# Dealing the mLSTM steps of a hybrid encoder block out at four places of a projection instead of one

## Chip, cores and metric

The kernel runs on one core of one Trainium2 chip. The time is the device time of one execution in microseconds, and 875.85 us is the median of three runs before the change (875.55 to 876.28).

## What is computed

One layer of a bidirectional encoder block on 512 tokens of width 1024, in fp32. From the normalised input come one combined projection, three token mixers (a chunkwise mLSTM in both directions, a 2-D neighbourhood attention, a cross-attention into 256 memory tokens), a gated merge, an output projection and a convolutional GLU feed-forward network. Cut to what the change touches:

```
h = rms_norm(x, mix_norm_g)
proj = h @ w_in      # mLSTM q,k,v,o,gates | attention q,k,v | memory q | merge gates
...
# mLSTM, one direction, per head and chunk: a = cumsum(log_f), D = a_j - a_s + log_i
m_j = max(a + m_prev, max_s D)
P = exp(D - m_j) * (q @ k.T)
num = P @ v + inter_w * (C_prev @ q)
den = sum(P) + inter_w * (n_prev @ q)
h = num / max(abs(den), exp(-m_j))
...
y_ml = sigmoid(o) * norm(h_fw + h_bw)
merged = g_ml * (y_ml @ w_br_ml) + g_na * (y_na @ w_br_na) + g_xa * (y_xa @ w_br_xa)
```

## The kernel before, in words

**Projections.** Every large matmul is done on a high and a low part of each operand: `mm3` (L212) issues three matmuls for each of the 8 tiles of 128 inputs, so a projection of 128 outputs for 512 tokens is 24 matmuls into one PSUM bank. `proj` (L395) does one such projection. Its weights come through `weights` (L201): SP loads blocks of 512 KB up to three ahead into three raw buffers, and one block ahead each block is split in two halves, the high part by ScalarE (L195, `wh`), the low part by VectorE (L196, `wl`). Four buffers of each kind hold two blocks, so a half can be split when its half of two blocks before is consumed. A raw buffer is free for SP's next load when its two L196 are done.

**Steps.** Between the projections the mLSTM is worked off in steps. `ml_all` (L652) is a generator whose `yield`s cut it in 27 pieces; `step(n)` (L1064) adds n to a quota and runs one piece for each whole number in it. Before the change a step call stands at the end of each projection, after its eviction from PSUM: `RB` = 1.25 for each of 16 projections in four groups of four (memory queries `xaq` L1080, output gates `o` L1086, neighbourhood queries and keys `naq`, `nak` L1119 and L1124), `RM` = 0.7 for eight shorter pieces of the memory keys and values between the second and third group. The gate projections that follow give half a step at their fourth tile and half at their end.

**What the pieces hold.** Piece 2: the transposes of the gate logarithms (L583) and the four scans over the tokens on VectorE (L589 to L601), two for the running maximum and two for the running sum. Piece 4: their difference `rr` (L607), written by POOL's queue to a buffer `rd` in DRAM (L609). Piece 5: transposes of the maxima (L614), the copy `lfc` (L618), the first loads of `R`, which is `rd` spread over all partitions (L660, on SP), and the transposes of the keys of head 0 (L681). Piece 6: `states` (L711) of head 0, the matmuls of keys with weighted values (L722 and `mm3` on the tile `u`). Then, for each head, `weights_J` (L742: key-query product L748, the exponential of `R` on ScalarE L752, their product `E` on VectorE L753) and, one piece later, `values_J` (L756: L761, L763 and a `mm3`); in the last piece of a head the keys of the next one; then the next states. `emit_y` (L802) transposes a finished head (L806).

**Deferred operations.** Pieces put work that may wait in the list `late`; `flush` (L390) emits it, and `proj` calls `flush` after its second tile. Among it are `spread` (L621: the maxima at chunk ends by L627, small sums, the exponentials L644 to L646), `weigh` (L697: the values times the state weights, L700, L703, L704), the masks added to `R` (`mask`, L664) and the products at the edges (`edges`, L668: L673 exponentiates `R`, L675 multiplies).

**Order.** Each engine works its own instructions in a fixed order. Within the order in which the program text emits them, the compiler's scheduler may move instructions of one engine past each other, so the order on an engine is not that of the text. `mem_part` (L484) loads a piece of the memory tokens (`memT`, SP), squares it (L489), splits it (L219, L220) and sums (L496); it stands at the end of each `xaq` projection, before its step.

Of the kernel before, what the change touches and what calls it, by code (L numbers as in the profile page):

```python
# [29 lines left out]
RM, RB = 0.7, 1.25  # L30
# [80 lines left out]
def hybrid_block(ctx, tc, xg, xT, memT, wflat, vecs, gbias, nabias, outa, outb, outc):  # L111
# [14 lines left out]
    def nm(s):  # L126
        uid[0] += 1
        return f"{s}_{uid[0]}"

    def unit(dt=F32):  # L130
        return up.tile([P, UNIT], dt, tag="unit", name=nm("u"))

    def scr(n=512):
        return sp.tile([P, S], F32, tag="scr", name=nm("s"))[:, :n]
# [4 lines left out]
    def mmps():  # L139
        return mmp.tile([P, 512], F32, tag="mm", name=nm("mm"))  # L140
# [60 lines left out]
    def weights(key):  # L201

        i, _, n = BINDEX[key]
        while st["raw"] <= min(i + RAW_AHEAD, len(BLOCKS) - 1):
            emit_raw(st["raw"])
            st["raw"] += 1
        while st["split"] <= min(i + SPLIT_AHEAD, len(BLOCKS) - 1):
            emit_split(st["split"])
            st["split"] += 1
        return split.pop(i)  # L210

    def mm3(ps, lh, ll, rh, rl, start, stop):  # L212
        PE.matmul(ps, lh, rh, start=start, stop=False)  # L213
        PE.matmul(ps, lh, rl, start=False, stop=False)  # L214
        st["mm"] = PE.matmul(ps, ll, rh, start=False, stop=stop).ins  # L215
# [89 lines left out]
    def folded(acc, ntok):  # L305

        lo, hi = slice(0, P // 2), slice(P // 2, P)
        t, parts = scr(ntok), sp.tile([P, S], F32R, tag="scr", name=nm("s"))[:, :ntok]
        A.activation(t[lo], acc[hi], AF.Copy)
        V.tensor_tensor(t[lo], acc[lo], t[lo], op=ALU.add)  # L310
        A.activation(parts[lo], t[lo], AF.Copy)
        V.tensor_tensor(parts[hi], t[lo], parts[lo].bitcast(F32), op=ALU.subtract)
        return (parts,)

    def square_sums(parts, ntok):

        ps = atps()
        for i, p in enumerate(parts):
            st["mm"] = PE.matmul(ps[:, :ntok], onesr, p, start=i == 0, stop=i == len(parts) - 1).ins
        return ps  # L320

    def rstd_cols(ps, ntok, tag, n=D):

        nt = ntok // P
        v, junk = tiny(nt), scr(P)
        for t in range(nt):
            V.tensor_tensor_reduce(junk, ps[:, t * P:(t + 1) * P], ident, 1.0 / n, 0.0, ALU.mult, ALU.add,
                                   accum_out=v[:, t:t + 1])
        col = cp.tile([P, nt], F32, name=f"rc_{tag}")
        st["pool"] = G.tensor_tensor(col, v, nhalf[:, :nt], op=ALU.pow).ins  # L330
        return col

    def rstd_wide(ps, ntok, tag, n=D):

        v, y = scr(ntok), scr(ntok)
        rb = cp.tile([P, ntok], F32, name=f"rb_{tag}", tag=f"rb{ntok}", bufs=1) if tag else scr(ntok)
        A.activation(v, ps[:, :ntok], AF.Ln, scale=1.0 / n)
        A.activation(y, v, AF.Exp, scale=-0.5)
        V.scalar_tensor_tensor(v, ps[:, :ntok], -0.5 / n, y, op0=ALU.mult, op1=ALU.mult)
        V.tensor_tensor(v, v, y, op=ALU.mult)  # L340
        V.scalar_tensor_tensor(rb, v, 1.5, y, op0=ALU.add, op1=ALU.mult)
        return rb
# [3 lines left out]
    XH = [hx[k // 4 * 2][:, (k % 4) * S:(k % 4 + 1) * S] for k in range(KT)]  # L346
    XL = [hx[k // 4 * 2 + 1][:, (k % 4) * S:(k % 4 + 1) * S] for k in range(KT)]
# [42 lines left out]
    def flush():  # L390

        while late:
            late.pop(0)()

    def proj(key, XHs, XLs, n=S, at={}, ps=None):  # L395

        ws = weights(key)
        k0 = 0 if ps is None else 1
        if ps is None:
            ps = mmps()  # L400
        for k in range(k0, KT):
            mm3(ps[:, :n], ws[k][0], ws[k][1], XHs[k], XLs[k], k == 0, k == KT - 1)
            if k == 1:
                flush()
            if k in at:
                at[k]()
        return ps
# [35 lines left out]
    def x_norm():  # L443
        ps = square_sums(xsum, S)
        norm.extend([rstd_wide(ps, S, "x"), rstd_cols(ps, S, "x")])

    proj(("mlk", 0), XH, XL, ps=ps_k[0], at={3: x_norm})
    proj(("mlk", 1), XH, XL, ps=ps_k[1])
    rb, rc = norm
    SY.dma_start(gbf, gbias.partition_broadcast(P))  # L450
# [24 lines left out]
    for f in range(4):  # L475
        ps = ps_k[f] if f < 2 else proj(("mlk", f), XH, XL)
        silu2(kT, slice(f * S, (f + 1) * S), conv(ps, rb, "mlw", "mlb", 4 + f, 8))
# [6 lines left out]
    def mem_part(kp):  # L484

        t = scr()
        SY.dma_start(t.rearrange("p (k m) -> p k m", k=2), memT[:, 2 * kp:2 * kp + 2, :])
        sq = scr()
        A.activation(sq, t, AF.Square)  # L489
        for i in range(2):  # L490
            k = 2 * kp + i
            split_act(MH[k], ML[k], t[:, i * M:(i + 1) * M], vcol("mem_g", k))
            if k == 0:
                V.scalar_tensor_tensor(macc, sq[:, :M], EPS * D / P, sq[:, M:2 * M], op0=ALU.add, op1=ALU.add)
            elif k > 1:
                V.tensor_tensor(macc, macc, sq[:, i * M:(i + 1) * M], op=ALU.add)  # L496
# [7 lines left out]
    for c in range(3):  # L504
        n, nk = TMC[c], TMK[c]
        pss = [(mmps if c % 2 else atps)() for _ in range(NT)]
        for h in range(KT // nk):
            ws = weights(("tm", c, h))
            for t in range(NT):
                tsl = slice(t * P, (t + 1) * P)  # L510
                for k in range(nk):
                    kk = nk * h + k
                    ps = pss[t][:, :n]
                    mm3(ps, XH[kk][:, tsl], XL[kk][:, tsl], ws[k][0], ws[k][1], kk == 0, kk == KT - 1)
        for t in range(NT):
            ps = pss[t]
            if c == 0:
                V.scalar_tensor_tensor(Gt[:, t, :], ps[:, :16], rc[:, t:t + 1], gb, op0=ALU.mult, op1=ALU.add)
            if c < 2:
                o = 16 if c == 0 else 0  # L520
# [543 lines left out]
    def step(n=1):  # L1064
        quota[0] += n
        while quota[0] >= 1 and gens:
            try:
                next(gens[0])
                quota[0] -= 1
            except StopIteration:  # L1070
                gens.pop(0)
        if not gens:
            quota[0] = 0.0
# [2 lines left out]
    so = []  # L1076
    gens.append(ml_all())

    xq = unit()
    for f in range(4):  # L1080
        ps = proj(("xaq", f), XH, XL)
        V.tensor_tensor(xq[:, f * S:(f + 1) * S], ps, rb, op=ALU.mult)
        mem_part(f)
        step(RB)
    for f in range(4):
        ps = proj(("o", f), XH, XL)  # L1086
        t = scr()
        V.tensor_tensor(t, ps, rb, op=ALU.mult)
        A.activation(t, t, AF.Tanh, scale=0.5)
        if f == 0:  # L1090
            so.append(unit())
            msum = folded(macc, M)
        if f == 1:

            with tc.issue_after(st["mm"]):
                mps = square_sums(msum, M)
            mrb, mrc = rstd_wide(mps, M, "m"), rstd_cols(mps, M, "m")
        V.tensor_scalar(so[0][:, f * S:(f + 1) * S], t, 1.0, None, op0=ALU.add)
        step(RB)
    mkv = unit()  # L1100
    mk, mv = mkv[:, 0:1024], mkv[:, 1024:2048]
    for f in range(4):
        ps = proj(("memk", f), MH, ML, M)
# [13 lines left out]
    nq, nk = unit(), unit()  # L1117
    rv = lambda a: a.rearrange("p (r b c) -> p b r c", r=ROWS, b=4)
    for f in range(4):  # L1119
        ps = proj(("naq", f), XH, XL)  # L1120
        V.tensor_tensor(nq[:, f * S:(f + 1) * S].rearrange("p (b r c) -> p b r c", r=ROWS, b=4), rv(ps), rv(rb),
                        op=ALU.mult)
        step(RB)
    for f in range(4):  # L1124
        ps = proj(("nak", f), XH, XL)
        V.scalar_tensor_tensor(nk[:, f * S:(f + 1) * S], ps, 0.125, rb, op0=ALU.mult, op1=ALU.mult)
        step(RB)

    mg = []
    mgv = lambda f: mg[f // 4][:, (f % 4) * S:(f % 4 + 1) * S]  # L1130
# [7 lines left out]
    for br in range(3):  # L1138
# [19 lines left out]
        for fp in range(4):  # L1158
# [9 lines left out]
            for i in range(2):  # L1168
                f = 2 * fp + i
                ps = mmps()  # L1170
# [22 lines left out]
    for f in range(KT):  # L1193
        xr = scr()
        SY.dma_start(xr, xT[f])
        ps = proj(("out", f), GH, GL)
# [145 lines left out]
    for hh in range(2):  # L1342
# [3 lines left out]
        for j in range(HF):  # L1346
            f = HF * hh + j
            if f == 0:
# [8 lines left out]
                k = KT - 1  # L1357
# [18 lines left out]
        for f in range(KT if hh == 0 else LF - 1):  # L1376
            ws = weights(("dn", hh, f, 0)) + weights(("dn", hh, f, 1))
            ps = mmps()
# [128 lines left out]
```

## Time and profile before

| | us |
|---|---|
| median of three runs | 875.85 |
| the profiled execution | 875.7 |
| its span on the core | 873.9 |
| TensorE busy | 868.1 |
| VectorE busy | 594.2 |
| ScalarE busy | 472.7 |
| GpSimd busy | 125.2 |

In the rows of the profile, PE is TensorE's matmuls, PEld its weight loads, DVE VectorE, ACT ScalarE, POOL GpSimd and SP the queue that issues most loads; a q behind the name marks the issue of a transfer. A row of a timeline has the start in us from the beginning of the span, the time of the group in us, the engine, the line of the kernel, the operation, the tiles (out<-in), shapes and the count of instructions merged into it. In brackets stands the idle time before it and what ended it. The time of a group of matmuls runs to the end of the last one, while the next may start earlier, since matmuls are pipelined; for the pace, starts are compared.

### The profile page before, as it was taken

The page shows a single profiled execution, that of the slowest core. Times are in us where ns is not written, and L with a number is a line of the kernel's source. Part 1 is how long each engine was busy: PE and PEld are TensorE (multiplying, and loading weights), DVE is VectorE, ACT ScalarE, POOL GpSimd, SP SyncE. Part 2 cuts the span into 40 slices and gives each one's busy share as a digit, 9 for nine tenths or more (in the row PEclk, how much of TensorE's full clock was granted, in tenths as well). Part 3 has the DMA queues.
Part 4 walks back from the last instruction along what each step waited for, and adds up shares of the span by engine and source line. Part 5 has one row for each costly group of instructions (what it writes and reads, how often), then busy time and mean ns, then how long its engine had stood idle before and what let it go on. Part 6 is the DMA issues. An engine that isn't in the chain of part 4 may idle for free.

```text
span 873.9 us, 12229 instructions
## 1 busy us (share of the span) xinstructions
PE 868.1 (99%) x4303; PEld 736.2 (84%) x4303; DVE 594.2 (68%) x1240; ACT 472.7 (54%) x996; POOL 125.2 (14%) x201
## 2 busy tenths in 40 slices
PE   9999999999999999999999999999999999999997
PEld 7898888888888888888888888888888888888887
DVE  7794789886677758897676658776633466666534
ACT  7563567765456658888544455444422344444532
POOL 0101100000163370600000002111100011111010
PEclk9999999999999999999999999999999999999999
DMA  8224633422242353533223432222233222222412
GB/s 281 99 77 148 210 123 125 166 82 90 95 132 81 111 161 108 158 120 122 98 97 109 145 108 97 97 97 96 76 100 104 107 97 97 97 97 90 142 34 97
DMA packets 39421, 99.81 MB, mean 114 GB/s; under 512 B 5688, under 2 KB 13880, under 8 KB 39360
## 3 DMA queue, kind: packets, MB, share of 16 engines
q1 hardware_dynamic: 31568, 92.32, 30.7%
q0 software_dynamic: 7360, 6.32, 3.2%
q8 instruction: 34, 0.56, 0.3%
q10 hardware_dynamic: 432, 0.39, 0.1%
q14 instruction: 27, 0.22, 0.1%
HBM read 94.80 MB, written 4.21 MB: 113 GB/s over the span
## 4 chain that ended last, share of the span: by engine, by line
PE 94%; DVE 3%; ACT 1%; issue 1%; DMA 1%; POOL 0%; POOLq 0%; SPq 0%
PE mm L214 28%; PE mm L213 28%; PE mm L215 28%; PE at L214 2%; PE at L215 2%; PE at L213 2%; PE at L938 1%; PE at L919 1%; PE at L761 1%; DMA R<-rd 1%; DVE wl L196 0%; PE at L900 0%; PE at L901 0%; PE at L1026 0%; PE at L243 0%
## 5 line engine op out<-in xcount | busy, mean ns | idle before, releaser
L213 PE MATMUL mm<-u,wh 128*128 128x512 f32 (+1 forms) x1072 | 414.6, 387 | 0.0
L215 PE MATMUL mm<-u,wl 128*128 128x512 f32 (+1 forms) x1072 | 411.9, 384 | 0.0
L214 PE MATMUL mm<-u,wh 128*128 128x512 f32 (+1 forms) x1072 | 411.6, 384 | 0.0
L195 ACT ACTIVATE wh<-wr 128x512 fp32r<-128x512 f32 (+2 forms) x298 | 183.9, 621 | 213.5 <-PE mm L214 168.2
L196 DVE TENSOR_TENSOR wl<-wr,wh 128x512 fp32r<-128x512 f32 (+3 forms) x300 | 203.9, 681 | 89.5 <-ACT wh L195 86.7
L215 PEld LDWEIGHTS mm<-u,wl 128*128 128x128 f32 x1072 | 201.4, 188 | 40.0
L213 PEld LDWEIGHTS mm<-u,wh 128*128 128x128 f32 x1072 | 201.6, 188 | 38.6 <-ACT wh L195 0.2
L214 PEld LDWEIGHTS mm<-u,wh 128*128 128x128 f32 x1072 | 201.6, 188 | 38.4
L1371 POOL TENSOR_TENSOR s<-s,rb 128x512 f32<-128x512 f32 x22 | 38.1, 1732 | 403.4 <-DVE s L1370 239.0
L542 POOL DMA_DIRECT2D u<-nav_d x128 | 62.5, 533 | 66.2 <-PE at L938 23.0
L219 ACT ACTIVATE u<-s 128x512 fp32r<-128x512 f32 x26 | 16.4, 632 | 57.7 <-DVE s L1374 56.2
L1374 DVE TENSOR_TENSOR s<-mm,s 128x512 f32<-128x512 f32 x22 | 15.2, 690 | 23.8 <-POOL s L1371 23.8
L462 ACT ACTIVATE s<-pad,vec 128x512 f32<-128x512 f32 x30 | 24.4, 813 | 9.4 <-DVE pad L460 9.4
L220 DVE SCALAR_TENSOR_TENSOR u<-s,u 128x512 fp32r<-128x512 f32 x26 | 19.1, 733 | 14.1 <-ACT u L219 14.0
L463 DVE SCALAR_TENSOR_TENSOR s<-pad,vec,s 128x512 f32<-128x512 f32 x30 | 22.5, 750 | 5.4 <-ACT s L462 5.2
L1370 DVE SCALAR_TENSOR_TENSOR s<-s,s 128x512 f32<-128x512 f32 x22 | 15.2, 692 | 13.4 <-ACT s L1369 13.3
L464 DVE SCALAR_TENSOR_TENSOR s<-pad,vec,s 128x512 f32<-128x512 f32 x30 | 22.5, 750 | 0.9
L1369 ACT ACTIVATE s<-s 128x512 f32<-128x512 f32 x22 | 13.9, 632 | 14.9 <-DVE s L1368 14.9
L460 DVE TENSOR_TENSOR pad<-mm,rb 128x512 f32<-128x512 f32 x22 | 15.1, 690 | 6.4 <-PE mm L215 6.2
L213 PE MATMUL mm<-wh,u 128*128 128x512 f32 x48 | 18.8, 392 | 0.0
L215 PE MATMUL mm<-wh,u 128*128 128x512 f32 x48 | 18.7, 390 | 0.0
L214 PE MATMUL mm<-wl,u 128*128 128x512 f32 x48 | 18.7, 390 | 0.0
(341 smaller groups left out, 1043.6 us busy)
## 6 DMA issues: line engine op xcount, KB each, us to landing
wr<-wflat SPq DMA_DIRECT2D x141, 512.0 KB, 3.2
nab<-nabias SPq DMA_DIRECT2D x16, 256.0 KB, 2.6
u<-nav_d POOLq DMA_DIRECT2D x128, 32.0 KB, 2.6
s<-xT SPq DMA_DIRECT2D x15, 256.0 KB, 3.7
wr<-wflat SPq DMA_DIRECT2D x14, 192.0 KB, 2.3
nav_d<-nv POOLq DMA_DIRECT2D x8, 256.0 KB, 3.0
R<-rd SPq DMA_DIRECT2D x8, 256.0 KB, 4.6
wr<-wflat SPq DMA_DIRECT2D x2, 544.0 KB, 3.1
```

What stands on the lines that cost most here:

```text
L195: A.activation(h[:, u:v], src, AF.Copy)
L196: V.tensor_tensor(l[:, u:v], src, h[:, u:v].bitcast(F32), op=ALU.subtract)
L213: PE.matmul(ps, lh, rh, start=start, stop=False)
L214: PE.matmul(ps, lh, rl, start=False, stop=False)
L215: st["mm"] = PE.matmul(ps, ll, rh, start=False, stop=stop).ins
L219: A.activation(h, src, AF.Copy, scale=scale)
L220: V.scalar_tensor_tensor(l, src, scale, h.bitcast(F32), op0=ALU.mult, op1=ALU.subtract)
L462: A.activation(t1, pad[:, 0:512], AF.Identity, scale=vcol(w, i), bias=vcol(b, i))
L463: V.scalar_tensor_tensor(t1, pad[:, 1:513], vcol(w, n + i), t1, op0=ALU.mult, op1=ALU.add)
L464: V.scalar_tensor_tensor(t1, pad[:, 2:514], vcol(w, 2 * n + i), t1, op0=ALU.mult, op1=ALU.add)
L542: G.dma_start(vw[r * 32:(r + 1) * 32, i * 256:(i + 1) * 256], nav_v[hf, r, CW[b]:CW[b] + 32, hp * 256:(hp + 1) * 256])
L1371: G.tensor_tensor(c, c, rb2, op=ALU.mult)
```

## The change

The 16 projections of the four groups call `step` with a quarter of 1.25 at four places, behind their second, fourth and sixth tile and at the end, where the eviction and (for `xaq`) `mem_part` stand before it as they did. And `flush` is called after the second, fourth and sixth tile in every projection that goes through `proj`, ahead of a step at the same tile. Nothing that is computed changes.

```diff
         for k in range(k0, KT):
             mm3(ps[:, :n], ws[k][0], ws[k][1], XHs[k], XLs[k], k == 0, k == KT - 1)
-            if k == 1:
+            if k in (1, 3, 5):
                 flush()
             if k in at:
                 at[k]()
...
+    def paced(key):
+        return proj(key, XH, XL, at={k: lambda: step(RB / 4) for k in (1, 3, 5)})
+
     xq = unit()
     for f in range(4):
-        ps = proj(("xaq", f), XH, XL)
+        ps = paced(("xaq", f))
         V.tensor_tensor(xq[:, f * S:(f + 1) * S], ps, rb, op=ALU.mult)
         mem_part(f)
-        step(RB)
+        step(RB / 4)
...
     for f in range(4):
-        ps = proj(("nak", f), XH, XL)
+        ps = paced(("nak", f))
         V.scalar_tensor_tensor(nk[:, f * S:(f + 1) * S], ps, 0.125, rb, op0=ALU.mult, op1=ALU.mult)
-        step(RB)
+        step(RB / 4)
```

The groups `o` and `naq` change in the same two lines.

More of the change, by code (lines that the diff above doesn't have):

```diff
@@ L1077, in hybrid_block @@
     gens.append(ml_all())
+    def paced(key):
+        return proj(key, XH, XL, at={k: lambda: step(RB / 4) for k in (1, 3, 5)})
     xq = unit()
     for f in range(4):
-        ps = proj(("xaq", f), XH, XL)
+        ps = paced(("xaq", f))
         V.tensor_tensor(xq[:, f * S:(f + 1) * S], ps, rb, op=ALU.mult)
         mem_part(f)
-        step(RB)
+        step(RB / 4)
     for f in range(4):
-        ps = proj(("o", f), XH, XL)
+        ps = paced(("o", f))
         t = scr()
@@ L1119, in hybrid_block @@
     for f in range(4):
-        ps = proj(("naq", f), XH, XL)
+        ps = paced(("naq", f))
         V.tensor_tensor(nq[:, f * S:(f + 1) * S].rearrange("p (b r c) -> p b r c", r=ROWS, b=4), rv(ps), rv(rb),
                         op=ALU.mult)
-        step(RB)
+        step(RB / 4)
     for f in range(4):
-        ps = proj(("nak", f), XH, XL)
+        ps = paced(("nak", f))
         V.scalar_tensor_tensor(nk[:, f * S:(f + 1) * S], ps, 0.125, rb, op0=ALU.mult, op1=ALU.mult)
-        step(RB)
+        step(RB / 4)
     mg = []
```

## The prediction

> **What bounds the kernel now.** I read the page first: its busy times and the granted clock.
>
> ```profile
> span 873.9 us, 12229 instructions
> ...
> PE 868.1 (99%) x4303; PEld 736.2 (84%) x4303; DVE 594.2 (68%) x1240; ACT 472.7 (54%) x996; POOL 125.2 (14%) x201
> ...
> PEclk9999999999999999999999999999999999999999
> ```
>
> TensorE is busy for 868.1 of 873.9 us at full clock. The change neither adds nor removes a matmul, so all it can win are stalls of TensorE, and all it can lose are new ones. The second view was who waited for whom, for the weight loads of TensorE (total us, times, longest), and the third TensorE's order in time around the longest of these waits.
>
> ```profile
> PEld at L761 <- DVE E L753: 1.1, 3, 0.6
> ```
>
> ```profile
> 142.33 0.39 PE L748 MATMUL at<-u,u 128*128 128x128 f32 x2
> 142.55 0.60 PE L681 MATMUL at<-ident,u 128*128 128x128 f32 x4
> ...
> 143.56 0.71 PE L761 MATMUL at<-u,E 128*128 128x129 f32 x4 [0.41 <-DVE E L753]
> ...
> 186.98 0.71 PE L761 MATMUL at<-u,E 128*128 128x129 f32 x4
> ```
>
> The reader is to see three small stalls in the whole stretch of mLSTM steps, all before the value matmuls (L761), all for the weights E that VectorE multiplies (L753). At 142.55 two steps stand back to back behind the fourth output-gate projection. Two rows of L748 take 0.22 us, so one of these small matmuls takes 0.11, and four L681 end at 142.99; L761 starts at 143.56. **That is 0.57 us lost,** and a further 0.1 inside the L761 group (0.71 for four, where four L681 take 0.60). The group at 186.98 loses the same 0.1; the third wait of the row is its twin one head later, taken at 0.1 too. In all about 0.9 us.
>
> **The change, part by part.** *Where the steps go.* Before, a projection adds 1.25 to the quota and 20 steps fall at the ends of 16 projections, four ends taking two. Now a quarter, 0.3125, is added behind tiles 2, 4, 6 and 8. Counting the quota through gives the same 20 steps in the same order, each 0 to 6 tiles earlier; a tile is three matmuls. The four pairs come apart. The deferred operations are emitted behind tiles 2, 4 and 6.
>
> *What it wins.* The third step of head 0 moves from the end of its projection to behind the second tile, and its E is needed 18 matmuls later, not at once. The two later pairs come apart the same way. I count the whole 0.9 us as won. In the changed program's order the fp32 bursts between the projections' matmuls number 29, as before, so nothing is won or lost by switching between kinds of matmul.
>
> *How fast TensorE runs.* Its timeline, with the bursts that frame the steps:
>
> ```profile
> 104.42 0.60 PE L583 MATMUL at<-ident,lfc 128*100 128x128 f32 x4
> ...
> 115.77 0.51 PE L614 MATMUL at<-ident,s 100*128 100x100 f32 x4
> ...
> 117.94 0.53 PE L627 MATMUL at<-lfc,ident 128*128 128x32 f32 x4
> ...
> 122.48 0.38 PE L722 MATMUL at<-s 128*128 128x129 f32 x2
> ...
> 123.07 0.28 PE L213 MATMUL at<-u 128*128 128x258 f32 x1
> 123.18 0.28 PE L214 MATMUL at<-u 128*128 128x258 f32 x1
> ...
> 178.98 0.39 PE L722 MATMUL at<-s 128*128 128x129 f32 x2
> ```
>
> Between 104.42 and 115.77 lie two projections, 48 matmuls, and one burst of four (0.44): 10.9 / 48 = 0.227 us each. So six tiles are 4.1 us, four 2.7, two 1.4.
>
> *The scans and what is behind them.* Step 2 (transposes L583, then four scans on VectorE) moves two tiles up: L583 starts at about 103.05. VectorE before, cut to the scans and the stretch up to L607:
>
> ```profile
> 105.94 1.22 DVE L589 TENSOR_TENSOR_SCAN s<-s,at 4x512 f32<-4x512 f32 x1
> ...
> 110.88 0.69 DVE L196 TENSOR_TENSOR wl<-wr,wh 128x512 fp32r<-128x512 f32 x1
> ...
> 113.79 0.68 DVE L196 TENSOR_TENSOR wl<-wr,wh 128x512 fp32r<-128x512 f32 x1
> 114.39 0.42 DVE L496 TENSOR_TENSOR acc_m<-acc_m,s 128x256 f32<-128x256 f32 x1
> 114.73 0.87 DVE L220 SCALAR_TENSOR_TENSOR u<-s,vec,u 128x256 fp32r<-128x256 f32 x2
> 115.52 0.41 DVE L496 TENSOR_TENSOR acc_m<-acc_m,s 128x256 f32<-128x256 f32 x1
> 115.85 0.68 DVE L607 TENSOR_TENSOR s<-cu,s 36x512 f32<-36x512 f32 x1
> ```
>
> From start to start an L196 or an eviction takes 0.60, an L496 0.34, an L220 0.40, the four scans 4.94. ScalarE and the two queues:
>
> ```profile
> 105.06 0.59 ACT L585 ACTIVATE s<-at 36x512 f32<-36x512 f32 x1
> ...
> 115.80 0.63 ACT L195 ACTIVATE wh<-wr 128x512 fp32r<-128x512 f32 x1 [0.94 <-PE mm L214]
> 116.33 0.49 ACT L618 ACTIVATE lfc<-at 128x400 f32<-128x400 f32 x1
> ...
> 119.61 0.23 ACT L644 ACTIVATE wt<-wt 128x32 f32<-128x32 f32 x1 [0.43 <-DVE wt L638]
> ...
> 122.59 0.40 ACT L673 ACTIVATE ee<-R,mt 128x128 f32<-128x128 f32 x1 [0.81 <-DMA R<-rd]
> 124.50 0.40 ACT L673 ACTIVATE ee<-R,mt 128x128 f32<-128x128 f32 x1 [1.52 <-DMA R<-rd]
> 124.81 0.61 ACT L195 ACTIVATE wh<-wr 128x512 fp32r<-128x512 f32 x1
> ```
>
> ```profile
> 105.94 0.33 SPq L159 DMA_DIRECT2D wr<-wflat  x1
> 106.32 0.42 SPq L487 DMA_DIRECT2D s<-memT  x1
> ...
> 118.59 0.33 SPq L660 DMA_DIRECT2D R<-rd  x1
> ```
>
> L585 ran 0.64 behind L583, so now at 103.7; the scans run from 104.3 to 109.25. In the changed order these stand behind the scans, ahead of L607: two evictions, three L196, four L220, four L496. 5 x 0.60 + 4 x 0.40 + 4 x 0.34 = 5.96, so L607 starts at about 115.2. **Its step moved up by six tiles, 4.1 us, but the instruction moves by only 0.6,** because earlier scans push evictions, weight splits and memory preparation in front of it.
>
> One of these L196 is the low half for the end of the fourth query projection. It ended before 105.94 and will end near 112.0, since it now waits behind the scans; its reader, 14 matmuls into a projection that starts at 115.77 - 24 x 0.227 = 110.3, wants it at 113.5, so TensorE does not stall. It also frees the raw buffer that SP waits for: the weight load at 105.94 and the load of memT behind it (106.32) go out at about 112.1 and 112.5. By the page's list of loads
>
> ```profile
> s<-memT SPq DMA_DIRECT2D x4, 256.0 KB, 3.9
> ```
>
> memT lands at 116.4. What ScalarE makes of it, one 512-wide instruction (0.53, as the L195 at 115.80) and two of 256 (0.40, as VectorE's L220), now stands before L618, which starts at 117.7 instead of 116.33 and ends at 118.2. Its reader L627 ran at 117.94, so TensorE may lose 0.3 us there. I cost it at nothing, because the next stall ends at a time that R sets and absorbs it; without that stall it would be 0.3.
>
> *The wait that takes over.* L607 feeds two writes to rd in POOL's queue, then R is loaded (118.59, waited for until 122.59). From L607's start to R's arrival is 6.74 us; from 115.2 that is 121.95. Before, L673, the first reader of R, stood behind the exponential of the state weights (L644), and the scaling of the values by them (L703, L704). In the changed order L673 and one weight split (L195) stand **ahead** of L644 on ScalarE, and the mask of R (L666) ahead of L700 and L704 on VectorE. So what is queued behind R is all that head 0's state matmuls (L722, L213 to L215 on u) wait for. L673 starts at 121.95; to the next instruction it takes 0.31 (124.50 to 124.81), the L195 0.53 (115.80 to 116.33): L644 starts at 122.8 instead of 119.61. From L644 to the end of the last L704 it was
>
> ```profile
> 120.34 1.30 DVE L704 SCALAR_TENSOR_TENSOR u<-u,wt,u 128x129 fp32r<-128x129 f32 x4
> ```
>
> 121.64 - 119.61 = 2.03, and I allow 0.1 for L645, moved up between the L703. Last L704: 124.93. Its reader is the L214 that ran at 123.18. **Stall 1.8 us,** split over L722, L213 and L214.
>
> The arrival of R is the one price that is not fixed. Eight loads of R, from issue to landing (min, median, max):
>
> ```profile
> DMA to landing us min/median/max: 3.0/4.6/5.7
> ```
>
> The one in question took 4.0 (118.59 to 122.59); at 3.0 the stall is 0.8, at 5.7 it is 3.5. I take 4.0, since it is the same load, first of its four and alone on the queue when issued.
>
> *What costs nothing.* Steps 7 to 10 and 16 to 25: E was ready at once or is needed at least 12 matmuls (2.7 us) after the instruction that starts it, which covers an exponential and an L753. The tightest is head 2's state step, four tiles up: its L722 goes from 178.98 to 176.25, and what it needs last was done at
>
> ```profile
> 175.10 0.35 DVE L704 SCALAR_TENSOR_TENSOR u<-u,wt,u 128x129 fp32r<-128x129 f32 x1
> ```
>
> 175.45, so 0.8 us to spare; a stall starts if the split runs that much later. On SP three loads of R now pass one weight load, which is needed two projections later (10.9 us).
>
> *Sum.* 1.8 - 0.9 = +0.9 us. The profiled execution took 875.7 (span 873.9 and 1.8 around it), 0.15 under the median of the three runs. 875.85 + 0.9 = **876.8 us,** +0.1%; 0.2% is 1.75 us, about what a measurement of this kernel tells from no change.
>
> **The rivals.**
>
> *R is not in the way.* The step that writes rd moved 4.1 us up in the program; if VectorE reaches L607 by then, R lands at about 118.5, L673 has nothing to wait for, and only the 0.9 is left: 875.0. For it: VectorE has idle time elsewhere (68% busy). Against: the sum of 5.96 us of work between scans and L607, which is fixed by order.
>
> *R lands as late as the slowest load: slower.* Same place as the forecast, the state matmuls of head 0. At 5.7 us from issue the stall is 3.5, less 0.9: +2.6, 878.4. It decides from a landing 4.9 us after issue, where the net loss passes 1.75. For it: the four loads of R now leave back to back; the second, which had others around it, landed at 124.50. Against: the first was issued ahead of the others then and is now.
>
> *Nothing moves.* TensorE takes the same matmuls in the same number of bursts, and stall and gain cancel: 875.85. For it: both are under 0.2%. Against: the reordered queues.
>
> *The clock falls behind the stall.* The first matmuls of the run are slow:
>
> ```profile
> 0.77 3.15 PE L243 MATMUL at<-const-bfloat16-1.0 128*128 128x256 bf16 x14 [0.77 <-PEq L1494]
> ```
>
> 0.225 us for 256 columns, where 258 columns take 0.11 at 123.07. Half rate for the roughly 5 us that the start shows would lose 2.5 us: 879.3. Against: between 104 and 231 us the profile has no gap as long as the one that I forecast, so no row shows what one does. [...]
>
> **How the numbers follow.** Forecast 0.52, R not in the way 0.15, R late 0.18, nothing moves 0.12, clock 0.03. The forecast's own range is 875.8 (R after 3.0 us) to 877.6 (after 4.8). The range reaches on from 875.0 (no stall) to 878.4 (R at its slowest). Faster by over 0.2% needs 1.75 us won where I find 0.9: 0.03. Slower by over 0.2%: the late R, the clock, and a twelfth of the forecast's own spread, 0.18 + 0.03 + 0.04 = 0.25. Within: 0.72.
>
> **What would show it.** In the profile after, TensorE waits at L722, L214 or L215 on u near 122.5 to 125 for L700 or L704, and on ScalarE L673 waits about 2 us for R ahead of L644; L607 starts near 115.2; the waits of L761 for L753 are gone. The forecast is wrong if L673 shows no wait for R, if L607 is earlier than 114, if there is a stall behind 130 us, or if the granted clock drops.

## The result and the profile after

| | us |
|---|---|
| before, median of 6 runs | 876.14 (875.55 to 876.63) |
| after, median of 6 runs | 879.0 (878.2 to 879.72) |
| ratio, with its 95% interval | 1.0032 (1.0019 to 1.0045) |
| the profiled execution after, and its span | 878.59, 876.8 |

The change makes the kernel 2.9 us slower, three times the forecast loss and outside the forecast range. The page of the kernel after, its span and busy times:

```profile
span 876.8 us, 12222 instructions
...
PE 869.2 (99%) x4303; PEld 736.7 (84%) x4303; DVE 593.9 (68%) x1240; ACT 471.2 (54%) x996; POOL 125.4 (14%) x201
```

The matmuls are the same; the span is 2.9 us longer than the 873.9 of the profiled execution before. Who waited for whom, for the weight loads of TensorE between 98 and 265 us (us in total, times, longest):

```profile
PEld at L627 <- ACT lfc L618: 2.2, 1, 2.2
PEld at L722 <- PE mm L215: 0.6, 1, 0.6
PEld at L214 <- DVE u L704: 0.4, 1, 0.4
PEld at L213 <- ACT u L703: 0.2, 1, 0.2
```

The waits for E at L761 are gone, as forecast, and four waits near 120 us have come. TensorE's timeline there:

```profile
118.01 0.40 PE L215 MATMUL mm<-u,wl 128*128 128x512 f32 x1
120.16 0.63 PE L627 MATMUL at<-lfc,ident 128*128 128x32 f32 x4 [1.75 <-ACT lfc L618]
...
124.61 0.39 PE L215 MATMUL mm<-u,wl 128*128 128x512 f32 x1
125.21 0.46 PE L722 MATMUL at<-s 128*128 128x129 f32 x2 [0.21 <-DVE mt L643]
...
126.95 0.38 PE L722 MATMUL at<-ee,s 128*128 128x129 f32 x2
```

A matmul of 512 columns starts 0.23 us after the one before it. From 118.01 to 120.16 are 2.15, so 1.92 us are lost at L627. From 124.61 to 125.21 are 0.60, 0.37 lost; and the two L722 rows stand 1.74 apart, where before they were at 122.48 and 123.43, 0.95 apart: 0.79 lost. **The stalls add up to 3.1 us.** The forecast had 1.8, at the second place alone.

ScalarE after, the instructions on which those two places hang:

```profile
118.29 0.63 ACT L489 ACTIVATE s<-s 128x512 f32<-128x512 f32 x1 [4.29 <-DMA s<-memT]
...
119.62 0.48 ACT L618 ACTIVATE lfc<-at 128x400 f32<-128x400 f32 x1
...
123.58 0.40 ACT L673 ACTIVATE ee<-R,mt 128x128 f32<-128x128 f32 x1 [1.92 <-DMA R<-rd]
...
124.41 0.21 ACT L644 ACTIVATE wt<-wt 128x32 f32<-128x32 f32 x1
```

In brackets stand the two late transfers: the last piece of memT, for which L489 waits 4.29 us ahead of L618, and R, for which L673 waits 1.92 us ahead of L644. The chain of waits (start, us, what) says which of the two set the end:

```profile
115.62 0.61 DVE s L607
116.24 0.28 issue
116.52 3.09 DMA rd<-s
119.61 0.02 issue
119.63 3.87 DMA R<-rd
...
123.58 0.41 ACT ee L673
```

It runs through L607, the write of rd and the load of R, not through memT. VectorE's row of L607:

```profile
115.55 0.68 DVE L607 TENSOR_TENSOR s<-cu,s 36x512 f32<-36x512 f32 x1
```

And the transfers themselves, issued between 112 and 119 us after, in the view of the DMA queues (packets, MB and share; then count, KB each, us from issue to landing):

```profile
q8 instruction: 1, 0.02, 0.8%
...
s<-memT SPq DMA_DIRECT2D x1, 256.0 KB, 5.4
rd<-s POOLq DMA_DIRECT2D x2, 8.0 KB, 2.9
```

Before, the same load of memT took 3.5 us and the same writes of rd 1.7:

```profile
s<-memT SPq DMA_DIRECT2D x1, 256.0 KB, 3.5
```

```profile
rd<-s POOLq DMA_DIRECT2D x2, 8.0 KB, 1.7
```

The view gives the median of the two writes. The load of R waits for the first of them, and its time is in the chain above: 3.09 us. A weight load of 512 KB leaves SP ahead of the writes. Before, it leaves 2.3 us ahead of the first write (116.82); after, it is delayed and leaves 0.9 us ahead (116.52). SP's rows, before and after:

```profile
114.50 0.33 SPq L159 DMA_DIRECT2D wr<-wflat  x1
```

```profile
115.65 0.33 SPq L159 DMA_DIRECT2D wr<-wflat  x1
```

The stalls can be set against the whole stretch. Between the first transpose of the maxima (L614) and a group of transposes behind the sixteen projections (L1026) TensorE issues 757 matmuls, the same in each kernel below; kernel 4 and kernel 10 are those of experiments 4 and 10.

| kernel | L614 starts, us | L1026 starts, us | between |
|---|---|---|---|
| before | 115.77 | 252.54 | 136.8 |
| after | 116.07 | 255.44 | 139.4 |
| kernel 4 | 116.22 | 252.38 | 136.2 |
| kernel 10 (L618 and L1032 there) | 115.90 | 253.95 | 138.1 |

After, the stretch takes 2.6 us more than before, and 3.2 more than in kernel 4, which has no stall in it. So the stalls cost 3.2 (the 3.1 and 0.1 in small pieces), and the waits that are gone gave back 0.6. The remaining 0.3 of the 2.9 stands ahead of L614.

The times of the six runs go with the granted clock: 878.2 and 878.59 at a mean of 0.999 and 1.0, 878.99 to 879.72 at 0.997 and 0.998.

### The profile page after: what moved, and what is told of

Same layout as the page of the kernel before. It is cut to its first block, busy times and chain, and to the rows that moved or that the text cites. A ratio compares the mean times of both kernels' runs of the same rounds, so it can differ in the third digit from the quotient of the medians.

```text
span 876.8 us, 12222 instructions
## 1 busy us (share of the span) xinstructions
PE 869.2 (99%) x4303; PEld 736.7 (84%) x4303; DVE 593.9 (68%) x1240; ACT 471.2 (54%) x996; POOL 125.4 (14%) x201
## 4 chain that ended last, share of the span: by engine, by line
PE 97%; DVE 1%; DMA 1%; issue 0%; ACT 0%; POOL 0%; POOLq 0%; DVEq 0%; ACTq 0%
PE mm L215 28%; PE mm L213 28%; PE mm L214 28%; PE at L214 2%; PE at L215 2%; PE at L213 2%; PE at L938 1%; PE at L761 1%; PE at L919 1%; DMA R<-rd 0%; PE at L900 0%; PE at L901 0%; PE at L748 0%; PE at L1026 0%; PE at L243 0%
## 5 line engine op out<-in xcount | busy, mean ns | idle before, releaser
L213 PE MATMUL mm<-u,wh 128*128 128x512 f32 (+1 forms) x1072 | 415.1, 387 | 0.0
L215 PE MATMUL mm<-u,wl 128*128 128x512 f32 (+1 forms) x1072 | 411.8, 384 | 0.0
L214 PE MATMUL mm<-u,wh 128*128 128x512 f32 (+1 forms) x1072 | 411.7, 384 | 0.0
L196 DVE TENSOR_TENSOR wl<-wr,wh 128x512 fp32r<-128x512 f32 (+3 forms) x300 | 203.8, 681 | 94.7 <-ACT wh L195 91.3
L215 PEld LDWEIGHTS mm<-u,wl 128*128 128x128 f32 x1072 | 201.5, 188 | 40.2
L214 PEld LDWEIGHTS mm<-u,wh 128*128 128x128 f32 x1072 | 201.7, 188 | 38.7
L213 PEld LDWEIGHTS mm<-u,wh 128*128 128x128 f32 x1072 | 201.6, 188 | 38.2
L219 ACT ACTIVATE u<-s 128x512 fp32r<-128x512 f32 x26 | 16.4, 632 | 58.0 <-DVE s L1377 56.3
L213 PE MATMUL mm<-wh,u 128*128 128x512 f32 x48 | 18.8, 392 | 0.0
L215 PE MATMUL mm<-wh,u 128*128 128x512 f32 x48 | 18.7, 390 | 0.0
L214 PE MATMUL mm<-wl,u 128*128 128x512 f32 x48 | 18.7, 390 | 0.0
```

What stands on the lines that cost most here:

```text
L196: V.tensor_tensor(l[:, u:v], src, h[:, u:v].bitcast(F32), op=ALU.subtract)
L219: A.activation(h, src, AF.Copy, scale=scale)
```

## The experiments

Each kernel is compared with the kernel before on the same chip; its median there lay between 875.93 and 876.13. Edits are against the changed kernel where nothing else is said. Not tried on the chip: the more frequent `flush` alone. In the compiled order every engine's instructions stand the same with it and without it, in the kernel before and in the changed one, so the whole effect is that of the steps.

The main theory, 1, is that of the chain just read: R sets when head 0's state matmuls can run, and the wait for memT is only an earlier part of the same loss. Its first rivals are a cause outside these waits (2) and two stalls that add, with memT the larger (3).

### 1. R's readers behind the state weights

```diff
-                        A.activation(wh[j][:, ds], va[:, j + 1, h, 0:129], AF.Copy, scale=col)
+                        st["w703"] = A.activation(wh[j][:, ds], va[:, j + 1, h, 0:129], AF.Copy, scale=col).ins
...
-                edges(0, R, ee)
-                for d in range(2):
-                    mask(R, d)
+                with tc.issue_after(st["w703"]):
+                    with tc.issue_after(st["dve"]):
+                        edges(0, R, ee)
+                        for d in range(2):
+                            mask(R, d)
```

`issue_after` keeps what is issued in its block behind the named instruction on the same engine.

> The changed kernel, with the first readers of R (L673, L666 of head 0) held behind the state weights (L703, L704) on ScalarE and VectorE; nothing else moves. Theory 1 (R's arrival sets when head 0's state matmuls may run, memT's late landing only takes the first 1.9 us of that wait): the stalls at L722, L213 and L214 near 125 us (together about 1.2) go, the one at L627 (1.9) stays, -1.2: about 877.8. Theory 2 (the loss is the clock or the many bursts, not these waits): no change, 879.0.

Measured: 878.85, ratio 1.0034 (1.0023 to 1.0046). The waits at L722, L213 and L214 are gone from its trace, yet no time is won in most runs. The windows view of this kernel gives the reason (start and end, length, busy us and count of PE, PEld, DVE, ACT, POOL, granted clock, DMA share, GB/s):

```profile
119.00:120.00 1.00, 0.13 (x1) 0.13 (x2) 0.93 (x3) 1.00 (x5) 0.00 (x0) 1.00 0.00 0
...
120.00:121.00 1.00, 1.00 (x5) 1.00 (x6) 1.00 (x4) 0.80 (x3) 0.00 (x0) 0.50 0.43 113
121.00:122.00 1.00, 1.00 (x3) 0.80 (x3) 0.97 (x6) 0.37 (x1) 0.00 (x0) 0.50 0.82 162
122.00:123.00 1.00, 1.00 (x4) 0.72 (x3) 0.69 (x7) 0.00 (x0) 0.00 (x0) 0.50 0.86 160
123.00:124.00 1.00, 1.00 (x5) 0.82 (x4) 0.11 (x1) 0.77 (x3) 0.00 (x0) 0.80 0.89 231
```

Behind the stall at L627, here 2.0 us, the granted clock is 0.50 for some 3.4 us, and a large matmul starts 0.43 us after the one before it instead of 0.23:

```profile
121.66 0.63 PE L215 MATMUL mm<-u,wl 128*128 128x512 f32 x1
122.09 0.63 PE L213 MATMUL mm<-u,wh 128*128 128x512 f32 x1
```

Five of the six runs have a mean clock of 0.996 or 0.997 and take 878.76 to 880.74; the sixth, at 0.999, takes 877.39, 0.4 under the 877.8 that theory 1 expected. In the trace the slow stretch also moves L722 back by some 1.6 us, which by itself would cover a wait; the order on ScalarE (L644 ahead of L673) and the sixth run are the cleaner evidence. So the theory holds for the waits, and the clock, which the prediction gave 0.03, has its hand in the time.

### 2. memT's last load on another queue

```diff
-        SY.dma_start(t.rearrange("p (k m) -> p k m", k=2), memT[:, 2 * kp:2 * kp + 2, :])
+        (G if kp == 3 else SY).dma_start(t.rearrange("p (k m) -> p k m", k=2), memT[:, 2 * kp:2 * kp + 2, :])
```

> The changed kernel, with the fourth load of memT issued by GpSimd's queue instead of SP's, so that it no longer stands behind the weight load that waits for a raw buffer. Theory 1 (R sets the end): the stall at L627 goes (1.9 to under 0.3), but the state matmuls of head 0 still end their wait at about the same time, so the stalls at L722 to L214 grow from 1.2 to about 3, unless the write of rd now finds quieter DMA engines and R lands up to 1.3 us earlier: 877.7 to 879.0. Theory 3 (the two stalls add, memT is the main cause): -1.9, 877.1 and the stalls at L722 to L214 stay at 1.2.

Measured: 878.58, ratio 1.0029 (1.0017 to 1.0041). The waits of TensorE's matmuls in this kernel:

```profile
PE at L722 <- DVE mt L643: 2.1, 1, 2.1
PE at L214 <- DVE u L704: 0.2, 1, 0.2
```

L627 waits no more, and the stall at L722 has grown from 0.37 to 2.26; with the 0.79 behind it that is 3.05, where it was 3.08. **The two stalls do not add: R sets the end, and a wait ahead of it only takes a part of the same loss.** Theory 3 falls.

### 3. Both edits

> Both edits: R's readers behind the state weights and the fourth memT load on GpSimd's queue. Theories 1 and 3: no stall over 0.3 us is left between 115 and 130 us, and the won 0.9 us of the step pairs shows: 875.0 to 875.5. If a wait for E or the second readers of R takes over, 876 or more.

Measured: 875.86, ratio 0.9997 (0.9989 to 1.0006). Nothing waits near 120 us. A new wait of 0.7 us for a low weight split (L196) at 157 us takes most of the gain back.

### 4. The memory queries left as they were

```diff
-        ps = paced(("xaq", f))
+        ps = proj(("xaq", f), XH, XL)
...
         mem_part(f)
-        step(RB / 4)
+        step(RB)
```

> The changed kernel, but the four memory-query projections (xaq) take their step at the end as before (step(RB)); output gates, neighbourhood queries and keys stay dealt out in quarters, flush behind tiles 2, 4 and 6. Theories 1 and 3 (all of the loss comes from the steps dealt out in xaq): no stall at L627 or L722, the waits of L761 for L753 stay away: 875.0 to 875.4, below before. If the later groups cost something themselves, 876 or more.

Measured: **875.2, ratio 0.9990 (0.9981 to 0.9999)**, 0.93 us below the kernel before; the interval reaches from 0.1 to 1.7. No matmul waits between 98 and 265 us. All of the loss comes from the four xaq projections, and the gain stays without them. Of the 0.9 that the prediction counted as won, the trace shows 0.6 (the table above). This is the version to keep.

### 5. The scans alone moved up, in the kernel before

```diff
-        ps = proj(("xaq", f), XH, XL)
+        ps = proj(("xaq", f), XH, XL, at={5: lambda: step(0.75)} if f == 1 else {})
...
-        step(RB)
+        step(RB - 0.75 if f == 1 else RB)
```

> The kernel before, with one thing of the change: step 2 (transposes L583 and the four scans) comes behind the sixth tile of the second xaq projection instead of its end; all other steps where they were. Theory 4 (the scans ahead of the eviction and the low split are by themselves what delays the loads behind them): a stall of about 1.9 us at L627 or L722 as in the changed kernel, 878 and more. Theory 5 (it takes the scans, the load of memT queued behind the held-up weight load, and R's readers ahead of the state weights together; here memT stands ahead of that load and R's readers stay behind L704): no new stall over 0.5 us near 120 us, 876.0 to 876.6.

Measured: 875.55, ratio 0.9995 (0.9986 to 1.0004); no new stall. With the scans at 103.44, L607 runs only at 117.09, yet nothing waits for R, since its readers stand behind L704, and the memT loads have all left SP by 102.6. Theory 4 falls: early scans are harmless by themselves. In this trace L761 waits for L753 for 0.7 us in all, where it was 1.1 before, though the pairs of steps stand where they were. So that wait also changes in size, here by 0.4 us, without its steps being moved.

### 6. The scans alone put back, in the changed kernel

```diff
-        ps = paced(("xaq", f))
+        ps = proj(("xaq", f), XH, XL) if f < 2 else paced(("xaq", f))
...
-        step(RB / 4)
+        step(RB if f < 2 else RB / 4)
```

> The changed kernel, with step 2 alone put back to the end of the second xaq projection (the first two xaq projections take step(RB) at the end); steps 3 and 4 and all later ones stay where the change puts them. R's readers stay ahead of L644 on ScalarE, but L607 now stands one split and one sum behind the scans. Theory 1 (what decides is when L607 runs): L607 at about 112, R there by about 119, no stall at L627 or L722, 875.0 to 875.4. Theory 6 (R's readers ahead of the state weights cost by themselves): a stall of 1 to 3 us at L722 to L214, 876.2 to 878.

Measured: 875.83, ratio 0.9999 (0.9990 to 1.0008). VectorE and ScalarE of this kernel:

```profile
112.13 0.68 DVE L607 TENSOR_TENSOR s<-cu,s 36x512 f32<-36x512 f32 x1
```

```profile
120.98 0.69 ACT L673 ACTIVATE ee<-R,mt 128x128 f32<-128x128 f32 x2 [1.62 <-DMA R<-rd]
121.59 0.22 ACT L644 ACTIVATE wt<-wt 128x32 f32<-128x32 f32 x1
```

L607 runs at 112.13 as expected, 3.4 us earlier. The last load of memT leaves SP at 106.63, about as early as before (106.32), so both waits of the changed kernel are touched. ScalarE now waits for the second load of R, which lands at 120.9 and not 119, and TensorE still loses 0.6 us at L213 to L215. Both theories are half right: the early L607 takes away most of the loss, the place of R's readers decides the rest.

### 7. Both: scans back, and R's readers behind

> Step 2 back at the end of the second xaq projection, and R's readers behind the state weights; every other step dealt out as in the change. The stall of 0.62 at L213 to L215 near 123 us that the kernel with step 2 back alone showed comes from R's readers ahead of L644; without it 875.2, the same as with the four xaq projections left at their ends. If it stays near 875.8, something else was lost there.

Measured: 875.37, ratio 0.9991 (0.9982 to 1.0000). The 0.6 is gone.

### 8. Why the transfers are late: the weight load

The 512 KB load that SP issues at 115.65 is held behind the first two loads of R, those of head 0.

```diff
             emit_raw(st["raw"])
...
+            if "R" in st:
+                with tc.issue_after(st.pop("R")):
+                    emit_raw(st["raw"])
```

`st["R"]` is set at the loads of head 0, the second of which is the one that counts.

> The changed kernel, with the 512 KB weight load that SP issues at 115.65 us held behind the second load of R (about 120.5); it is split only about 10 us later. Theory 9 (that load is what slows the write of rd, 2.9 us instead of 1.7, and the last memT load, 5.4 instead of 3.5): R there about 1.2 us earlier, memT up to 1.9 us earlier; the stalls at L627 and at L722 to L214 together shrink from 3.1 to about 1.9, the sum of the prediction: 876.8 to 877.3, and the mean clock stays at 0.999 in more runs. Theory 10 (memT is slow because of the 512 KB load right ahead of it): the stall at L627 stays near 1.9 and only the one behind it shrinks, to under 0.3: 878, with the clock low in most runs.

Measured: 878.9, ratio 1.0030 (1.0018 to 1.0042). The transfers of this kernel:

```profile
q8 instruction: 1, 0.02, 0.9%
...
s<-memT SPq DMA_DIRECT2D x1, 256.0 KB, 5.3
...
rd<-s POOLq DMA_DIRECT2D x2, 8.0 KB, 1.7
```

The write of rd is back at 1.7, so that load was what slowed it. The load of memT is as slow as before (5.3): theory 9 holds for the write and not for memT. L627 still loses 1.8 us. The mean clock is 0.997 in four of the six runs and 0.998 in two; in the trace, one of 0.997, the granted clock is 0.50 from 120.8 to 124.2 us, and that eats what was won. No wait at L722 to L214 is left in this trace, but the slow clock moves them back by 1.6 us, so this trace doesn't show what would be left at full clock; experiment 10 does.

### 9. Why the transfers are late: an instruction fetch

The trace holds 16 landings for one load, as many as the profile counts DMA engines; they are read here as one for each engine's share, and the load has landed with the last. In the trace after, the shares of the memT load issued at 112.81 arrive at these times:

```
115.94 115.96 116.00 116.05 116.06 116.17 116.18 116.19
116.21 116.22 116.24 116.26 116.28 116.29 116.43 118.19
```

Fifteen are there by 116.43, and the forecast had 116.4; the last comes 1.76 us later. The one packet in the q8 row is a fetch of 16 KB of instructions, from 115.66, that occupies its DMA engine for 0.94 us. In the traces of experiments 1 and 8 such a fetch starts at 114.00 and 114.96, with the same load under way, and the last share lands 1.85 and 1.69 us behind the other fifteen. To move the fetch, the warm-up at the start gets more and shorter matmuls:

```diff
-    for _ in range(WARM):
-        PE.matmul(pw[:, :256], one[:, :P], one, start=True, stop=True)
+    for _ in range(2 * WARM):
+        PE.matmul(pw[:, :P], one[:, :P], one[:, :P], start=True, stop=True)
```

> The changed kernel; the 14 warm-up matmuls of 256 columns at the start (L243) become 28 of 128 columns, so that TensorE's instruction stream is 14 matmuls longer ahead of the rest and its 16 KB instruction fetch, at 115.66 us in the changed kernel, comes some 14 matmuls (about 3 us) earlier, ahead of the last memT load's data. Extra instructions, outputs as before. Theory 11 (the fetch occupies one of the 16 DMA engines for 0.94 us and that engine's share of memT lands 1.8 us after the other 15): memT lands at about 116.4 as the prediction had it, the stall at L627 falls from 1.9 to 0.3 or less; the write of rd stays slow (2.9) and R late, so the stalls at L722 to L214 take what is left, and the time stays at 877.5 to 879. Theory 12 (memT is slow through the load ahead of it, the fetch is chance): memT stays at 5 us or more, the stall at L627 at 1.9.

Measured: 877.69, ratio 1.0029 (1.0017 to 1.0041). The fetch moved to 109.2, further than expected, and memT lands 4.0 us after its issue, at 116.2:

```profile
s<-memT SPq DMA_DIRECT2D x1, 256.0 KB, 4.0
```

TensorE's waits in this kernel:

```profile
PE at L722 <- DVE mt L643: 1.4, 1, 1.4
PE at L627 <- ACT lfc L618: 0.3, 1, 0.3
PE at L214 <- DVE u L704: 0.2, 1, 0.2
```

L627 loses 0.5 us instead of 1.9 (0.3 was expected), and the rest has gone to L722, as in experiment 2. Theory 11 holds: the fetch is what makes memT late. Which engine the fetch took the trace doesn't tell, and why the share comes 1.76 us late for 0.94 us of fetching stays open. Four runs take 877.47 to 877.78, two with a mean clock of 0.998 take 879.5 and 879.9.

### 10. Both causes taken away

> Both: the fetch moved as in the run before, and the 512 KB weight load of 115.65 us held behind R's first loads. Theory 11 with theory 9: memT lands 3.5 to 4 us after its issue, the write of rd takes 1.7, so L627 waits 0.3 or less and the state matmuls of head 0 about 1.8: the sum that the prediction made, 876.8 to 877.2 where the clock stays up.

Measured: **877.13, ratio 1.0012 (1.0004 to 1.0021)**, with a clock of 0.999 or 1.0 in all eleven runs. ScalarE and TensorE of this kernel, whose lines behind L215 have moved by up to 6 (L679 is L673, L728 is L722, L219 is L215):

```profile
122.09 0.40 ACT L679 ACTIVATE ee<-R,mt 128x128 f32<-128x128 f32 x1 [2.44 <-DMA R<-rd]
...
122.92 0.21 ACT L648 ACTIVATE wt<-wt 128x32 f32<-128x32 f32 x1
```

```profile
122.58 0.39 PE L219 MATMUL mm<-u,wl 128*128 128x512 f32 x1
123.72 0.46 PE L728 MATMUL at<-s 128*128 128x129 f32 x2 [0.74 <-DVE mt L647]
...
125.46 0.38 PE L728 MATMUL at<-ee,s 128*128 128x129 f32 x2
```

R is there at 122.09 (forecast 121.95), L644 starts at 122.92 (122.8), and the stall is 1.14 - 0.23 + 1.74 - 0.95 = 1.70 us (1.8). This is the forecast's own stall. With the 0.6 us that the stretch wins, and 0.2 in small pieces, it makes the 1.3 us of the table above; on the same chip the medians are 1.2 apart (877.13 and 875.93).

### 11. What a stall does to the clock

Into the kernel of experiment 4 an idle time of TensorE is put at 194 us, ahead of the fourth naq projection: a small matmul waits for a ScalarE copy and GpSimd multiplies on a tile of its own, one of 128x64, one of 128x320, or two of these.

```diff
+            A.activation(idle[:, :2], ps[:, :2], AF.Copy)
+            for _ in range(1):
+                G.tensor_tensor(idle[:, :320], idle[:, :320], idle[:, :320], op=ALU.mult)
+            pd = atps()
+            with tc.issue_after(st["mm"]):
+                gate_ins = PE.matmul(pd[:, :32], ident, idle[:, :32], start=True, stop=True).ins
```

> The xaq_ends kernel (875.2), with an idle time put into TensorE ahead of the fourth naq projection: a small matmul there waits for one GpSimd multiply of 128x320 that waits for a ScalarE copy of the finished third projection. Extra work, outputs as before. From the 1.735 us of a 128x512 GpSimd multiply, about 1.1 us, with the copy and the hand-overs about 1.7 us of idle TensorE. Theory 7 (a short stall costs its length): 876.9, clock as before in all runs. Theory 8 (a stall of about 2 us already halves the granted clock for some 3.4 us, as the one trace showed): 876.9 in some runs, up to 878.6 in others, their mean clock 0.997 to 0.998.

> As before it, with two such GpSimd multiplies in a row: about 2.8 us of idle TensorE. Theory 7: 878.0, clock as before. Theory 8: about 1.7 us more than the stall in most runs, 879.7, mean clock 0.997.

> The xaq_ends kernel with a shorter idle time ahead of the fourth naq projection: the GpSimd multiply is 128x64 instead of 128x320. The longer one gave 2.35 us of idle TensorE; 256 columns less at 3.4 ns each (1.735 us for 512) leave about 1.5. If the clock needs about 2 us without work to fall, 875.2 + 1.5 = 876.7 in all runs, mean clock 0.999 or 1.0; if shorter stalls do it too, some runs lie at 878 with 0.997.

Measured, with kernel 4 at 875.2 for comparison; the stalls are those of the profiled executions:

| multiplies | stall, us | clock 0.998 and up | clock 0.997 and below |
|---|---|---|---|
| 128x64 | 1.9 | 877.04, 877.62, 877.87 | 879.19, 879.31, 879.39, 879.4, 879.62 |
| 128x320 | 2.4 | 877.53, 877.88, 878.23, 878.39 | 879.47, 879.49 |
| 2 of 128x320 | 3.2 | 878.44, 881.86 | 880.41, 880.68, 881.77 |

The first two rows fall in two heaps: the stall alone, and on the mean 1.9 and 1.5 us more. A mean of 0.998 can be either: the 877.87 has no fall in its trace, and the 881.86 has the same fall as in experiment 1 (198 to 202 us, same columns):

```profile
198.00:200.00 2.00, 2.00 (x6) 1.71 (x7) 0.00 (x0) 0.20 (x2) 0.00 (x0) 0.50 0.49 193
200.00:202.00 2.00, 2.00 (x8) 1.54 (x8) 0.00 (x0) 0.00 (x0) 0.00 (x0) 0.71 0.00 0
```

Theory 8 holds, and the shortest of the three, planned at 1.5 and come out at 1.9, does it in five of eight runs, by their mean clock of 0.997. Which execution it meets isn't settled by the length of the stall.

The clock's records in the traces say what may settle it. In every profiled execution the full-clock stretches last whole multiples of 3.413 us (34, 56, 199, 220, 254 or 255 of them; 254 are the 866.985 us before, 255 the 870.399 after), and each of the three falls lasts one, so these pieces can be counted through any trace. Where the clock fell, nearly all of TensorE's gap lies within one piece, and the fall is the next piece. In four traces with gaps of 1.7 to 2.2 us the edge of a piece cuts the gap, and the clock stayed up:

| trace | gap, us | of it in one piece and the next | clock falls |
|---|---|---|---|
| experiment 1, L627 | 1.84 | 1.84, 0 | yes |
| experiment 8, L627 | 1.62 | 1.62, 0 | yes |
| 2 of 128x320 | 2.99 | 2.90, 0.09 | yes |
| after, L627 | 1.75 | 0.26, 1.49 | no |
| 128x64 | 1.77 | 0.37, 1.40 | no |
| 128x320 | 2.19 | 1.62, 0.57 | no |
| experiment 2, L722 | 2.10 | 1.73, 0.37 | no |

The gaps here are the idle times in brackets, from the end of one matmul to the start of the next, and so shorter than the stalls. The author's estimate from these seven rows is that what counts is how much of a gap falls into one piece, with a limit that is not sharp: 1.62 us went with a fall, and 1.62 and 1.73 without one. The pieces lie differently in each execution (the first full-clock stretch begins 5.21 us into the span before and 6.03 after), which would make the fall a matter of chance from run to run. Experiments 9 and 10, with gaps of 1.40 (0.53 and 0.88 of it in two pieces) and 0.74, show no fall. All this is read from traces; no experiment moved the pieces.

## Why the prediction was wrong, point by point

- *What is won, 0.9 us:* right in place, too large in size. The waits of L761 for L753 are gone, but the stretch that holds them is only 0.6 us shorter in kernel 4, which has this part alone. The 0.93 by which its median is lower meets the 0.9 by luck; experiment 7, whose kernel has the twelve projections dealt out too and no wait, gained 0.57.
- *The scans and L607 at 115.2:* right. The profiled execution after is 0.3 us late already ahead of this stretch (L614 at 116.07, before 115.77), and L607 ran at 115.55.
- *R's readers ahead of the state weights, and head 0's state matmuls behind them:* right in place and mechanism. Experiment 1 changed that order alone and took these waits away; its run with the clock up is the clean case.
- *"From L607's start to R's arrival is 6.74 us":* **the step that failed, by its size.** It was 8.03 (115.55 to 123.58). The load of R took 4.0 as assumed. The prediction carried over the old duration of the write of rd without naming it as a term, and it grew from 1.7 to 2.9 us (3.1 for the first of the two writes, on which R's load waits), because the delayed weight load left SP at 115.65 and was under way beside it (experiment 8, with that load held back: 1.7). The 6.74 came from a stretch in which that load had left at 114.50, further ahead of the write. So the rival "R late" had the right place and the wrong leg of the trip.
- *"memT lands at 116.4", L627 may lose 0.3:* wrong by 1.8 us, through one of 16 shares, late beside an instruction fetch that the prediction didn't look for. The fetch was at 112.9 in the kernel before, when nothing was loading.
- *"the next stall ends at a time that R sets and absorbs it":* right (experiments 2 and 9).
- *The clock stays up, 0.03 for the rival:* wrong in four of the six runs, by their mean clock. The stall became longer than the forecast's and came in one piece of 1.9 us. No row of the profile before showed how long a stall has to be to lower the clock, and the 0.03 was the author's estimate. Stalls of about 1.9 us were enough in most runs of experiments 1 and 8 and in five of eight in the first row of experiment 11, while the 0.9 us of experiment 10, with 0.8 more in small pieces behind it, never did it. That the rival's 879.3 lies near the measured 879.0 is luck: it added 2.5 us for the clock to a stall of 1.8, and the stalls were the larger part.
- *No stall behind 130 us, nothing else moves:* right.

The account: 876.14 + 3.2 - 0.6 = 878.7, near the two runs with the clock up (878.2 and 878.59); the other four, with the lower clock, take 878.99 to 879.72, and the median of all is 879.0. No trace of those four was kept, so that their clock fell at this stall is taken from experiments 1 and 8, where the traces show it. With the two late transfers mended, the kernel took 877.13 where the forecast was 876.8. The forecast's range ended at 878.4 because it bounded the load of R from both sides, and the write of rd and the clock from neither.

## What to carry to other kernels

When an instruction moves up on a full engine, look at what it pushes back. Here the scans on VectorE, busy for 11.27 of 12 us between 104 and 116 us before, pushed back the L196 that release raw buffers: the weight load and the load of memT behind it left at 112.43 and 112.81 instead of 105.94 and 106.32, and the next weight load at 115.65 instead of 114.50. The price lay where that load crossed a small transfer that somebody waits for, the write of rd (2.9 us instead of 1.7), and where an instruction fetch of 0.94 us fell into the load of memT (5.4 instead of 3.5). Each leg of a round trip through memory (here 3.09 us for the write and 3.87 for the load) is a term with bounds of its own. Ask for each group of steps how much room the engine has that they land on: here twelve projections gained 0.6 us, with VectorE busy for 102.6 of the 134 us between 116 and 250 before, and four, in the full stretch ahead of them, lost 3.2.

## What the runs showed of the hardware

- Behind a stall of TensorE of 2.0 us (experiment 1, L627) the granted clock was 0.50 for some 3.4 us, and a matmul of 512 columns started 0.43 us after the one before it instead of 0.23. With a stall of 1.9 us, the shortest case of experiment 11, five of eight runs had a mean clock of 0.997 and took 1.9 us more than the other three. The full-clock stretches in the traces were 34 to 255 times 3.413 us long. In the three traces with a fall 1.62 to 2.90 us of the gap lay in one piece of 3.413 us; in four with gaps of 1.7 to 2.2 us, 1.40 to 1.73 us did, and the clock stayed up. A stall of 0.9 us, with 0.8 more spread over the matmuls behind it (experiment 10), went with a mean clock of 0.999 or 1.0 in eleven of eleven runs.
- A 16 KB fetch of instructions held one of the 16 DMA engines for 0.94 us, and the last of the 16 shares of a 256 KB load under way then landed 1.76 us after the other fifteen. Lengthening TensorE's instruction stream by 14 matmuls moved the fetch from 115.66 to 109.2 us, and the load landed in 4.0 us instead of 5.4.
- Two writes of 8 KB took 1.7 us (median) with a 512 KB load sent 2.3 us ahead of them, and 2.9 us with that load sent 0.9 us ahead.
